# A hybrid decoder trunk on one core: where the writes of in_proj's weight pairs stand in the DMA queue

## The chip, the cores and the metric

The kernel runs on one core of one Trainium2 chip. The metric is the device time of one execution in microseconds (us), taken as the median of several runs; lower is better. Before the change it is 2620.64 us, the median of 3 runs (2617.64 to 2624.98).

## The reference

Two decoder layers on a sequence of 1024 tokens with a model width of 1024, in float32. Each layer normalises its input, multiplies it with one wide matrix w_in, and splits the columns of the product among three token mixers that work on the same input: A, a recurrence with a matrix state per head (RWKV-7); B, attention over dilated windows; C, latent attention. Their outputs are put side by side, multiplied with w_out and added to the residual. Then a gated feed-forward network follows:

```
for l in range(DEPTH):
    h = rms_norm(x, attn_norm_g[l])
    pa, pb, pc = split_sizes(h @ w_in[l], (A_PROJ, B_PROJ, C_PROJ))
    ya = rwkv7_mixer(pa, ...); yb = dilated_mixer(pb, ...); yc = mla_mixer(pc, ...)
    x = x + concatenate([ya, yb, yc]) @ w_out[l]
    h = rms_norm(x, ffn_norm_g[l])
    x = x + (silu(h @ w_gate[l]) * (h @ w_up[l])) @ w_down[l]
return rms_norm(x, final_norm_g)
```

## The kernel before, in words

**Split products.** A matmul of two float32 arrays is made of three passes over rounded parts. Each operand is split into a high part (a cast to fp32r on ACT, tile `wh` for weights) and a low part (source minus high part, on POOL for the weights here, tile `wl`). `mm3` (L268) multiplies high with high, high with low and low with high and adds all in PSUM. A weight tile of 128x512 values with its two parts is a *pair*; each part has 256 KB.

**in_proj** (L1154) computes h @ w_in for one half of the sequence (512 tokens) after the other, hf = 0 and hf = 1. Each half needs 36 weight pairs of the layer, two for each of 18 column blocks. For 16 of the blocks, a pair serves 4 steps of 3 matmuls with 512 columns (tile `inp`); the four pairs of the blocks 13 and 14 serve the values of mixer B (tile `vB`). Both halves use the same weights. So for hf = 0 a raw tile `wr` is loaded from `w_in`, split, used, and the pair is also written to a DRAM array `pairs_in`; for hf = 1 the pair is read back from there and needs no split (`again`, L477, is true for those keys).

**Planner.** The program is written out by a list scheduler, `Flow` (L111). Every activity is a generator, a *strand*, with a priority (lower goes first). A strand says which engine it wants next ("pe", "act", "pool", "dve" or "dma"), waits for an event, or asks for buffers. `run` (L173) always takes the strand that can start earliest by the planner's clocks, and `op` (L215) moves the clock of the engine by an estimated cost. The order in which strands are taken is the order of the instructions on each engine, and on the chip each engine works through its own instructions in that order. DMAs are issued by SP, in the order of the plan; `dma` (L324) estimates 256 KB at 728 ns (360 bytes per ns) on one clock for all DMAs, and the landing 2000 ns behind it. A DMA that must wait for a split on the chip holds up those behind it in SP's order.

**Loader.** `loader` (L482) supplies the weights in the order of their use. Its strand `fetch` (priority 1) loads raw tiles, at most three that are not yet split (`raws`, NRAW). The loader's own strand (priority 2) takes the raw tile, a slot of the ring (`ring`, NW = 6 pairs) and two pages of SBUF (`gp`, 79 pages in all, which the whole layer shares), and does the split. For in_proj's first half it then asks for the DMA and queues two writes, sets the event `there[k]`, which the read-back waits for, and sets `W[k]`, which in_proj waits for. After that it turns to the next pair. `drop` (L622) frees the two pages and the ring slot behind the last matmul with the pair.

**What lies around.** In layer 0, in_proj starts with the program, and its first half is accompanied by the norm of the second half (tiles `hx`, `hhi`, `hlo`), the token shift (`raw`, `pa`) and the beginning of the recurrence, which all use DVE, ACT and POOL. In layer 1 the loader's first splits lie beside the last matmuls of layer 0.

Of the kernel before, what the change touches and what calls it, by code (L numbers as in the profile page):

```python
# [36 lines left out]
C_SPLIT = (0, 1)  # L37
ROPE_START = (0, 16)
NORM_START = 8

VEC = {}
_n = 0
# [189 lines left out]
def trunk(ctx: ExitStack, tc: tile.TileContext, xT, pos, vec, con, first, w_in, small, uq, uqr, ukv,  # L232
# [91 lines left out]
    def dma(out, in_, nbytes):  # L324

        s = F.cur
        start = max(s.at(), F.clock["dma"])
        F.clock["dma"] = start + max(450.0, nbytes / 360.0)
        nc.sync.dma_start(out=out, in_=in_)
        return F.clock["dma"] + 2000  # L330
# [8 lines left out]
    def f32(ap):  # L339
        return ap.bitcast(F32)  # L340
# [140 lines left out]

    def loader(items):  # L482

        there.update({k: Event() for k, _ in items if k[0] in pairs_dram})

        def keep(k):
            late, soon = room(4), room(1)
            at = k[1][0][1] if k[0] == "S" else k[1]
            return lambda: soon() if k[0] == "in" or at < at_layer[0] else late()

        def own(k):

            rest, ffn = keep(k), k[0] in "gusS"
            return lambda: room(3.2)() if ffn and 3.2 in reserve else rest()

        def parts(k, srcs):

            if k[0] != "S":
                return [(Event(), srcs)]
            n = range(len(k[1]))  # L500
            at = [(g, 0) for g in n] + [(g, b) for g in n for b in (1, 2)] + [(g, 3) for g in n]
            return [(Event(), srcs[g][b], g, b) for g, b in at]

        def pair(k):

            return pairs_dram[k[0]][k[1], k[3], k[4]]

        queue = [(k, [] if again(k) else parts(k, srcs), own(k)) for k, srcs in items]

        def fetch():  # L510
            for k, todo, keep in queue:
                for ev, part, *_ in todo:
                    yield Need([raws])
                    wr = yield from page(["gp"], "wr", keep=keep, of=3.2)
                    w, t = 0, 0.0
                    yield "dma"
                    for a in part:
                        n = a.shape[-1]
                        t = dma(wr[:, w:w + n], a, 512 * n)
                        w += n  # L520
                    F.set(ev, wr, t)

        def raw_free(wr):
            free(wr)
            F.give(raws)

        F.spawn(fetch(), 1)
        for k, todo, keep in queue:
            if again(k):
                yield there[(*k[:2], 0, *k[3:])]  # L530
                yield Need([ring])
                w = yield from pages(["gp"], ["wh", "wl"], F32R, keep, 3.2)
                at = pair(k)
                yield "dma"
                for i in range(2):
                    t = dma(f32(w[i]), at[i], 262144)
                F.set(W[k], w, t)
                continue
            if k[0] == "S":
                gs = []  # L540
                for g, key in enumerate(k[1]):
                    evs = {b: ev for ev, _, g_, b in todo if g_ == g}
                    gs.append(Operands(key, k[2], evs, todo[0][1][0].shape[-1], keep, raw_free))
                for r in k[2]:
                    for g in gs:
                        yield from g.make(r)
                continue
            wr = yield todo[0][0]
            yield Need([ring])
            wh, wl = yield from pages(["gp"], ["wh", "wl"], F32R, keep, 3.2)  # L550
            yield from split(wr, wh, wl, "pool")
            raw_free(wr)
            now = F.cur.at()
            if k[0] in pairs_dram:
                yield "dma"
                for i, w in enumerate((wh, wl)):
                    t = dma(pair(k)[i], f32(w), 262144)
                F.set(there[k], None, t)
            F.set(W[k], (wh, wl), now)

    class Operands:

# [56 lines left out]
                F.spawn(self.later(2, a12), 2)  # L619
                yield from self.out(3, self.s2, free)  # L620

    def drop(w):  # L622
        free(*w)
        F.give(ring)

    def units(key, a):

# [385 lines left out]
    def layer(l):  # L1013
# [140 lines left out]
        def in_proj():  # L1154
            for hf in range(2):
                order = IN_ORDER[hf]
                for n_, idx in enumerate(order):
                    if hf == 0 and n_ == NORM_START:
                        F.spawn(norm1(1), 4)
                    if l == 0 and (hf, n_) == ROPE_START:  # L1160
                        F.spawn(rope_tables(), 7)
                    if hf == 1 and idx == B_START:
                        F.spawn(b_mixer(), 4)
                    if idx == 13:
                        for tb in range(2):
                            t = yield from page(["gp"], "pBv", keep=room(0.5))
                            for t2 in range(2):
                                tk = slice((2 * tb + t2) * 128, (2 * tb + t2 + 1) * 128)
                                p = yield from bank("vB", 4)
                                for k in range(KD):  # L1170
                                    hk = yield h[hf][k]
                                    wh, wl = yield W["in", l, hf, 13 + k // 4, k % 4 // 2]
                                    s = slice((k % 2) * 256, (k % 2) * 256 + 256)
                                    yield "pe"
                                    mm3(p[:, 0:256], (hk[0][:, tk], hk[1][:, tk]), (wh[:, s], wl[:, s]), k == 0, k == KD - 1)
                                    if tb == 1 and t2 == 1 and k % 2 == 1:
                                        drop((wh, wl))

                                def vout(p=p, t=t, t2=t2, tb=tb):
                                    if hf or l:  # L1180
                                        yield "act"
                                        acopy(t[:, t2 * 256:(t2 + 1) * 256], p[:, 0:256])
                                    else:
                                        yield rms
                                        yield "dve"
                                        ts(t[:, t2 * 256:(t2 + 1) * 256], p[:, 0:256], y0[:, 2 * tb + t2:2 * tb + t2 + 1], None,
                                           ALU.mult, rate=1.04)
                                    free(p)
                                    if t2 == 0:
                                        return  # L1190
                                    if hf == 1:
                                        F.set(Bv[2 + tb], t)
                                        return
                                    yield "dma"
                                    done = dma(pj_dram[8 + tb], t, 262144)
                                    F.cur.last, F.cur.t = None, done
                                    free(t)
                                    F.set(Bv[tb], (pj_dram[8 + tb], 128))

                                F.spawn(vout(), 2)  # L1200
                        continue
                    p = yield from bank("inp", 4)
                    for k in range(KD):
                        hk = yield h[hf][k]
                        wh, wl = yield W["in", l, hf, idx, k // 4]
                        s = slice((k % 4) * 128, (k % 4) * 128 + 128)
                        yield "pe"
                        mm3(p, (wh[:, s], wl[:, s]), hk, k == 0, k == KD - 1)
                        if k % 4 == 3:
                            drop((wh, wl))  # L1210
                        if n_ == len(order) - 1:
                            free(*hk)
                    if idx < 8:
                        F.spawn(shifted(hf, idx, p), 2)
                    elif idx == 8:
                        F.spawn(evac_to(Kr[hf], p, hf, 7, 64, shifted(hf, 8, p, 64, 96)), 2)
                    else:
                        ev, slot = {9: (Bq[0], 0), 10: (Bq[1], 1), 11: (Bk[0], 2), 12: (Bk[1], 3), 15: (Cq[0], 4),
                                    16: (Cq[1], 5), 17: (Ckv, 6)}[idx]
                        F.spawn(evac_to(ev[hf], p, hf, slot), 2)  # L1220
            unreserve(0.5)
            F.set(in_done)
# [1481 lines left out]
```

## Time and profile before

| | before |
|---|---|
| median of 3 runs | 2620.64 us |
| the profiled execution, its own time | 2621.2 us |
| its span, first to last instruction | 2619.4 us |
| mean granted clock of TensorE | 0.983 of full speed |
| PE busy | 2533.5 us, 97% of the span |
| DVE, ACT, POOL busy | 1747.4, 1135.3, 1154.9 us |
| DMA | 417.55 MB, mean 159 GB/s |
| writes to pairs_in, and reads from it | 144 each, 256 KB each |

The profiled execution is one among the executions of the kernel; its span leaves out what lies before the first and behind the last instruction. "Idle" is time in which an engine has no instruction running. A wait is put down to the operation that ended last before the waiting instruction could start; where an engine is not what sets the end, its waits cost nothing by themselves. Lines such as L295, L301 and L329 are those of helpers (the copy on ACT, the two-operand operation, and the DMA), so a row is told apart by its tiles.

### The profile page before, as it was taken

The numbers are of one execution on the slowest core, as the hardware profiler recorded it, in microseconds if no ns is written. First come the engines' busy times: TensorE is split into PE (matmuls) and PEld (weight loads), VectorE is DVE, ScalarE is ACT, GpSimd is POOL, SyncE is SP. The second block draws the span as 40 slices with busy tenths as digits, with TensorE's granted clock in tenths as the row PEclk, the third lists the DMA queues.
The fourth block names the chain that finished last, engine by engine and source line by source line (L and its number), as shares of the span: only waits on it lengthen the run. The fifth ranks groups of instructions, "written<-read, shape, count | busy, mean of one in ns | idle before, by whom it ended". The sixth has DMA issues, their size and how long they took to land. (4 is left out here: it accounts for less than half of the span.)

```text
span 2619.4 us, 38866 instructions
## 1 busy us (share of the span) xinstructions
PE 2533.5 (97%) x13112; PEld 2030.1 (78%) x13112; DVE 1747.4 (67%) x3415; ACT 1135.3 (43%) x2313; POOL 1154.9 (44%) x914
## 2 busy tenths in 40 slices
PE   7899999999899999999999999999998999999998
PEld 6678765888688888888878787568887888888887
DVE  6856677764987657566567376677458877665566
ACT  6542475663434334323354326557544334333221
POOL 3513231366645444455553123214655544444660
PEclk9999998999999999999999999999999999999999
DMA  7662321135255434896485241201461545449851
GB/s 265 234 211 88 118 64 29 56 115 199 99 176 194 140 134 161 307 316 229 166 290 194 93 171 36 63 25 53 168 198 60 197 165 177 147 136 351 291 196 65
DMA packets 235800, 417.55 MB, mean 159 GB/s; under 512 B 27600, under 2 KB 45264, under 8 KB 235472
## 3 DMA queue, kind: packets, MB, share of 16 engines
q1 hardware_dynamic: 235600, 415.07, 46.6%
q8 instruction: 103, 1.69, 0.3%
q14 instruction: 97, 0.79, 0.1%
HBM read 269.60 MB, written 141.69 MB: 157 GB/s over the span
## 5 line engine op out<-in xcount | busy, mean ns | idle before, releaser
L301 POOL TENSOR_TENSOR wl<-wr,wh 128x512 fp32r<-128x512 f32 (+1 forms) x304 | 436.5, 1448 | 387.0 <-ACT wh L295 310.2
L266 PE MATMUL gu<-hhi,wh 128*128 128x512 f32 x1232 | 483.7, 393 | 22.8 <-ACT u L295 16.5
L266 PE MATMUL gu<-hlo,wh 128*128 128x512 f32 x1232 | 481.1, 390 | 0.0
L266 PE MATMUL gu<-hhi,wl 128*128 128x512 f32 x1232 | 481.0, 390 | 0.0
L266 PEld LDWEIGHTS gu<-hhi,wh 128*128 128x128 f32 x1232 | 232.3, 189 | 79.6 <-ACT u L295 18.1
L295 ACT CAST wh<-wr 128x512 fp32r<-128x512 f32 (+1 forms) x424 | 244.4, 593 | 77.3 <-POOL wl L301 21.4
L266 PEld LDWEIGHTS gu<-hhi,wl 128*128 128x128 f32 x1232 | 232.3, 189 | 48.6
L266 PEld LDWEIGHTS gu<-hlo,wh 128*128 128x128 f32 x1232 | 232.4, 189 | 47.7
L301 POOL TENSOR_TENSOR wl<-s,wh 128x512 fp32r<-128x512 f32 (+1 forms) x136 | 181.5, 1342 | 197.1 <-ACT wh L295 142.8
L266 PE MATMUL dn<-bhi,wh 128*128 128x512 f32 (+1 forms) x664 | 252.0, 380 | 0.0
L266 PE MATMUL dn<-blo,wh 128*128 128x512 f32 (+1 forms) x664 | 251.5, 379 | 0.0
L266 PE MATMUL dn<-bhi,wl 128*128 128x512 f32 (+1 forms) x664 | 251.2, 379 | 0.0
L266 PE MATMUL inp<-hhi,wh 128*128 128x512 f32 x512 | 213.9, 418 | 11.4 <-ACT wh L295 11.4
L295 ACT CAST wh<-s 128x512 fp32r<-128x512 f32 (+1 forms) x204 | 116.8, 581 | 247.0 <-DVE s L301 199.7
L266 PE MATMUL inp<-hhi,wl 128*128 128x512 f32 x512 | 205.6, 401 | 5.2 <-POOL wl L301 5.2
L266 PE MATMUL inp<-hlo,wh 128*128 128x512 f32 x512 | 204.9, 400 | 1.2 <-DVE hlo L310 1.2
L301 DVE TENSOR_TENSOR x<-x,dn 128x512 f32<-128x512 f32 (+1 forms) x160 | 104.6, 657 | 109.3 <-PE dn L266 86.7
L301 DVE TENSOR_TENSOR v<-u,gu 128x512 f32<-128x512 f32 x132 | 90.1, 682 | 126.4 <-PE gu L266 126.2
L301 POOL TENSOR_TENSOR v<-v 128x512 f32<-128x512 f32 x66 | 98.0, 1488 | 134.3 <-DVE v L301 133.4
L291 ACT ACTIVATE P<-P,mx 128x512 f32<-128x512 f32 (+1 forms) x192 | 117.5, 613 | 63.9 <-DVE mx L857 42.5
L266 PEld LDWEIGHTS dn<-bhi,wh 128*128 128x128 f32 x664 | 124.9, 188 | 23.5
L266 PEld LDWEIGHTS dn<-bhi,wl 128*128 128x128 f32 x664 | 124.9, 188 | 23.4
(319 smaller groups left out, 5403.6 us busy)
## 6 DMA issues: line engine op xcount, KB each, us to landing
act_dram<-ahi SPq DMA_DIRECT2D x142, 256.0 KB
act_dram<-alo SPq DMA_DIRECT2D x142, 256.0 KB
bhi<-act_dram SPq DMA_DIRECT2D x142, 256.0 KB
blo<-act_dram SPq DMA_DIRECT2D x142, 256.0 KB
wr<-in_w_gate_dram SPq DMA_DIRECT2D x104, 256.0 KB
wr<-in_w_up_dram SPq DMA_DIRECT2D x104, 256.0 KB
wr<-in_w_in_dram SPq DMA_DIRECT2D x72, 256.0 KB
pairs_in<-wh SPq DMA_DIRECT2D x72, 256.0 KB
```

Of the source, the lines that this page charges most:

```text
L266: nc.tensor.matmul(out=out, lhsT=lhsT, rhs=rhs, start=start, stop=stop, **kw)
L291: nc.scalar.activation(out=out, in_=in_, func=func, **kw)
L295: nc.scalar.copy(out=out, in_=in_)
L301: ENG[eng].tensor_tensor(out=out, in0=a, in1=b, op=op)
```

## The change

After a split the loader no longer queues the two writes itself. It starts a strand of its own for them, `put` with priority 2, which begins 4000 ns behind the estimated end of the split, and goes on to the next pair. `drop` gets the pair's key: a pair that is written to DRAM is freed only when its write's estimated landing has passed, by a strand `drop_put`. `there` now holds only the keys that are written, so that pairs read back for the second half are freed as before.

```diff
+PUT_DELAY = 4000.0
@@ loader
-        there.update({k: Event() for k, _ in items if k[0] in pairs_dram})
+        there.update({k: Event() for k, _ in items if k[0] in pairs_dram and not again(k)})
@@
+        def put(k, w):
+            F.cur.after(F.cur.t + PUT_DELAY)
+            yield "dma"
+            for i in range(2):
+                t = dma(pair(k)[i], f32(w[i]), 262144)
+            F.set(there[k], None, t)
@@
             yield from split(wr, wh, wl, "pool")
             raw_free(wr)
-            now = F.cur.at()
             if k[0] in pairs_dram:
-                yield "dma"
-                for i, w in enumerate((wh, wl)):
-                    t = dma(pair(k)[i], f32(w), 262144)
-                F.set(there[k], None, t)
-            F.set(W[k], (wh, wl), now)
+                F.spawn(put(k, (wh, wl)), 2)
+            F.set(W[k], (wh, wl))
@@
-    def drop(w):
+    def drop(w, k=None):
+
+        if k in there:
+            F.spawn(drop_put(w, k), 2)
+            return
         free(*w)
         F.give(ring)
+
+    def drop_put(w, k):
+        yield there[k]
+        drop(w)
@@ in_proj
-                                        drop((wh, wl))
+                                        drop((wh, wl), ("in", l, hf, 13 + k // 4, k % 4 // 2))
@@
-                            drop((wh, wl))
+                            drop((wh, wl), ("in", l, hf, idx, k // 4))
```

## Rows read from the trace of the kernel before

**Rows 1.** The page, part 1: busy us of each engine (share) xinstructions.
```profile
PE 2533.5 (97%) x13112; PEld 2030.1 (78%) x13112; DVE 1747.4 (67%) x3415; ACT 1135.3 (43%) x2313; POOL 1154.9 (44%) x914
```

**Rows 2.** Busy us by stage; the last three: granted clock, DMA share, GB/s.
```profile
8.70:140.00 131.30, 117.78 (x571) 92.82 (x572) 102.66 (x200) 70.94 (x125) 66.92 (x54) 0.96 0.75 259
...
300.00:500.00 200.00, 193.35 (x1106) 132.24 (x1105) 147.37 (x444) 126.75 (x309) 64.86 (x61) 0.95 0.12 36
1290.00:1430.00 140.00, 135.56 (x692) 111.60 (x691) 103.72 (x210) 71.79 (x127) 74.15 (x57) 1.00 0.71 246
1600.00:1800.00 200.00, 189.85 (x1105) 129.16 (x1104) 140.49 (x442) 123.80 (x306) 62.69 (x59) 0.96 0.12 35
```

**Rows 3.** PE's waits, 8.7 to 140 us: us in total, times, longest.
```profile
PE inp L266 <- ACT wh L295: 11.4, 3, 8.7
PE inp L266 <- POOL wl L301: 5.2, 5, 2.1
```

**Rows 4.** Timeline of PE: start, us, operation, [idle before <-releaser].
```profile
33.09 0.50 PE L266 MATMUL inp<-hhi,wh 128*128 128x512 f32 x1 [1.42 <-ACT wh L295]
...
34.45 0.50 PE L266 MATMUL inp<-hhi,wl 128*128 128x512 f32 x1 [0.63 <-POOL wl L301]
...
102.71 0.50 PE L266 MATMUL inp<-hhi,wl 128*128 128x512 f32 x1 [2.13 <-POOL wl L301]
...
106.52 0.50 PE L266 MATMUL inp<-hhi,wh 128*128 128x512 f32 x1 [1.20 <-ACT wh L295]
...
109.09 0.80 PE L266 MATMUL inp<-hhi,wl 128*128 128x512 f32 x1 [1.84 <-POOL wl L301]
109.69 0.63 PE L266 MATMUL inp<-hhi,wh 128*128 128x512 f32 x1
...
114.81 0.41 PE L266 MATMUL inp<-hhi,wh 128*128 128x512 f32 x1
```

**Rows 5.** Busy us by stage of 20 us, columns as in rows 2.
```profile
100.00:120.00 20.00, 14.72 (x67) 10.78 (x66) 16.61 (x23) 7.02 (x12) 14.90 (x12) 0.83 0.56 194
120.00:140.00 20.00, 19.67 (x134) 17.95 (x132) 17.67 (x48) 5.16 (x8) 11.29 (x10) 1.00 0.97 335
```

**Rows 6.** Timeline of SP's DMA queue: start, us of issue, target<-source.
```profile
22.31 0.42 SPq L329 DMA_DIRECT2D wr<-in_w_in_dram  x1
...
24.79 0.89 SPq L329 DMA_DIRECT2D tabs<-in_con_dram  x1
...
90.93 0.42 SPq L329 DMA_DIRECT2D wr<-in_w_in_dram  x1
...
112.85 0.44 SPq L329 DMA_DIRECT2D wr<-in_w_in_dram  x1
...
139.17 0.73 SPq L329 DMA_DIRECT2D wh<-pairs_in  x1
```

**Rows 7.** Timeline of ACT: the casts of the 7th, 25th and 29th weight.
```profile
32.44 0.60 ACT L295 CAST wh<-wr 128x512 fp32r<-128x512 f32 x1
...
105.85 0.61 ACT L295 CAST wh<-wr 128x512 fp32r<-128x512 f32 x1
...
116.04 0.62 ACT L295 CAST wh<-wr 128x512 fp32r<-128x512 f32 x1 [0.67 <-DMA wr<-in_w_in_dram]
```

**Rows 8.** Timeline of POOL: the subtractions from 101.39 and from 128.24 us.
```profile
101.39 1.27 POOL L301 TENSOR_TENSOR wl<-wr,wh 128x512 fp32r<-128x512 f32 x1
...
128.24 2.56 POOL L301 TENSOR_TENSOR wl<-wr,wh 128x512 fp32r<-128x512 f32 x2 [4.63 <-DMA pairs_in<-wh]
```

**Rows 9.** Waits of SP's DMA queue, 8.7 to 140 us, columns as in rows 3.
```profile
SPq L329 <- ACT wh L295: 34.3, 19, 4.0
SPq L329 <- POOL wl L301: 21.4, 19, 2.6
```

**Rows 10.** ACT's waits for the loads, 8.7 to 140 us.
```profile
ACT wh L295 <- DMA wr<-in_w_in_dram: 7.4, 6, 2.2
```

**Rows 11.** Stages of PE's operations on tile inp alone.
```profile
0.00:148.70 148.70, 99.44 (x382) 0.97 0.77 262
```

## The prediction

> **What bounds the kernel now.** I read the page's busy shares first: PE is busy 2533.5 of 2619.4 us [rows 1], so only 85.9 us of idle can be won anywhere. Next the table by stage: in 8.7 to 140 us (layer 0, first half of in_proj) PE is busy 117.78 of 131.30 us, idle 13.5; in layer 1's like stage (1290 to 1430) it is idle 4.4 of 140 [rows 2]. Both stages make and write 36 weight pairs, so what the change can remove directly lies in the first. Then PE's waits in 8.7 to 140: 11.4 us for the cast wh and 5.2 us for the subtraction wl [rows 3]. Of the 11.4, 8.7 is the start of the program, before any weight exists, and stays. That leaves 2.7 + 5.2 = 7.9 us in which PE stood because a weight pair was not split yet. PE's timeline puts them: 1.42 us before 33.09 and 0.63 before 34.45 (2.05), then 2.13 before 102.71, 1.20 before 106.52 and 1.84 before 109.09 (5.17); the rest, 0.7, is in crumbs [rows 4]. After the last of these the matmuls start 0.427 us apart instead of 0.227 (12 starts between 109.69 and 114.81), the lower of the clock's two levels, 1.2 GHz: 12 x 0.2 = 2.4 us more [rows 4]; the granted clock from 100 to 120 us is 0.83 [rows 5].
>
> **Why the splits were late.** The seventh load of a weight was issued at 22.31, and its cast began only at 32.44; the 25th was issued at 90.93 and cast at 105.85 [rows 6, 7]. Where a cast does wait for its load, issue to cast is 3.2 us (112.85 to 116.04) [rows 6, 7]. So these weights had lain in SBUF some 7 and 11 us. It was the written order of ACT and POOL, not the DMA, that held them. In the code the loader strand asks for the DMA turn after each split, and only when the planner's DMA clock comes round goes on to the next split. Where the planner thinks its DMA backed up, other strands' work gets ahead of the cast. At 24.79 a transfer of 1088 KB was queued [rows 6]; at the planner's 360 bytes/ns that is 3.1 us of backlog, as an estimate, and the cast at 32.44 came behind ACT's work for the token shift.
>
> **The change part by part.**
> *Loader goes on at once.* No DMA turn between two splits. In the backed up opening that moves casts forward; I take the 2.05 us stall at 31.7 to 34.5 as gone. At 100 to 109 the DMA was busy only 0.56 [rows 5], so there the turn itself can hardly have held the loader. There POOL starts the subtraction at 101.39 without a gap before it, busy with other operations, and ACT casts only at 105.85 though its load had come long before [rows 7, 8]. These 5.17 us fall only if the loader comes to this place with more pairs in hand: the ring holds six, and two more pairs (2 x 12 matmuls x 0.227 = 5.4 us of PE work) would cover it. Bounds: 0 (same order, same stall) and 5.17 + 2.4 of clock. Loads (priority 1) now pass puts (priority 2) whenever the planner's DMA is backed up, so the lead should grow between 10 and 60 us; I take the full 7.6, the end that this priority speaks for.
>
> *Writes 4 us later.* The 144 writes of both layers stay, with the same bytes; nothing is saved on the 16 DMA engines. On SP's queue each write stood at the moment of its split: SP waited 34.3 us for wh and 21.4 for wl before 140 us [rows 9], and every load behind a write waited too. Those 55.7 us are no PE time: the casts waited for loads only 7.4 us in all [rows 10]. In layer 1 PE's idle in the like stage is only 4.4 us [rows 2], so I put layer 1 at 0; half of that idle, +-2, are the bounds.
>
> A rule of the Trainium skill would make more of this: "DMA: Bandwidth & Descriptors", section "Anatomy of one DMA — SWDGE (gpsimd) path", says that DMA engines never wait on semaphores, the issuing sequencer does before dispatch. By it all 55.7 us of SP's waits are time in which loads stood undispatched, and the sum would be some of that, up to the whole 13.5 us of idle. The trace agrees on where the wait sits, but its casts show that the loads were in time anyhow.
>
> *Pairs held for the write.* drop now waits for the put's estimated end, so a ring slot is kept at least 4.0 (delay) + 2 x 0.73 + 2.0 (the planner's figures) = 7.5 us behind the split. Six slots over 7.5 + 2 us of split give a pair each 1.6 us; the stage takes 131.3 / 36 = 3.6 us a pair. So the ring doesn't bind, until puts queue more than some 12 us behind.
>
> *Read-back for the second half.* The first read of a written pair was issued at 139.17 [rows 6], with the DMA 0.97 busy at 335 GB/s before it [rows 5]. Its first use is near 148.7: by then 382 of the first half's 384 matmuls of this form have started [rows 11], so the slack is about 9 us. That read needs a ring slot, and the last six pairs now hold theirs until their puts land. The pair six from the end is subtracted from 128.24, two in 2.56 us [rows 8], so it is split at 129.5. If nothing queues: 129.5 + 4.0 + 1.6 (0.52 MB at 335 GB/s) + 3.2 (landing as above) = 138.3, no loss. If all six puts queue: 129.5 + 4.0 + 6 x 1.6 + 3.2 = 146.3, read landed at 149.5, 0.8 us late. If the first half ends 9 us sooner the slack goes down by as much. Bounds 0 and 9; I take 0.7, since the slots' hold begins earlier too when the splits do.
>
> *The rest of the plan.* Every strand behind is planned anew. What this can do I bound by two stretches of equal work in different surroundings: 300 to 500 us is idle 6.65, 1600 to 1800 idle 10.15 [rows 2], 3.5 apart. I take 0, +-3.5 for one such stretch and +-6 for the kernel.
>
> **The sum**, against the profiled execution's own 2621.2 us (span 2619.4 and 1.8 around it): -2.05 - 5.17 - 2.4 + 0.7 = -8.9, so 2612.3. The median shown, 2620.64, is 0.56 below the profiled execution, so the forecast is **2612 us**, 0.33% faster.
>
> **The rivals.**
> *The stalls at 100 to 109 stay.* For: DMA busy 0.56 and weights long landed, so what orders ACT and POOL there is norm and recurrence work. Against: more lead from the opening. It keeps -2.05 and gives 0.7 back: 2619.
> *The change does not do what it says.* SP runs ahead of the estimated clock; if the chip lags the plan by more than 4 us, SP reaches the put before the split has ended and waits as now. For: plan and chip run apart freely. Against: the put is then behind loads that were planned after the split, so these are out already. 2620.6, no change.
> *ACT stands at casts (slower).* With no DMA turn between, a cast is planned at the load's estimated landing, 0.73 + 2.0 = 2.7 us behind issue, while the rows show 3.2 where a cast truly waited. ACT is in order, so 0.5 us and more at each cast falls on the evacuations and the recurrence behind it. Place: 10 to 140 us. Today 6 of 36 casts wait, 7.4 us in all, 1.2 each [rows 10]. If half of all 36 wait that long, 18 x 1.2 - 7.4 = 14 us of ACT; ACT is busy 70.94 of 131.3 us [rows 2], so perhaps two thirds of it, 9 to 10 us, reach PE, with the old stalls kept: 2630. It decides once PE's lead at these casts is under one pair (2.7 us). Against: the loads leave SP earlier too, no longer behind the puts.
>
> The same page of the Trainium skill, section "Latency and other measured facts", speaks for this rival: it puts HBM access at 0.2 us on average and 2 us at high load. No run here shows the memory's share alone; by it a landing could be near 2 us later than planned rather than 0.5, and the 18 casts would cost the more.
>
> **How the numbers follow.** Forecast (about 2612, faster) 0.42. Stalls stay 0.27 and no effect 0.10, both within 0.3%, which is 7.9 us and about what a measurement of this kernel can tell from no change. ACT stands at casts, or a late read-back with the new plan on top, 0.21, slower. So faster 0.42, same 0.37, slower 0.21. The forecast's own range is 2605 (the median less all 13.5 us of idle and 2.4 of clock) to 2618 (only the 2.05 won). The range that holds the time 8 times in 10 takes in the plan's -6 on the fast side, 2599 (2605 - 6), and the slow rival's 2630.
>
> **What would show it.** In the profile after: loads on SP's timeline no longer between a wh write and a wl write of the same pair, and SP's 55.7 us of waits for wh and wl mostly gone. PE's waits for wh and wl in 8.7 to 140 fall from 16.6 to under 10. The granted clock of 100 to 120 us is 1.00 instead of 0.83. The first read-back stands near 130 to 140 us with no PE wait at the second half's first matmuls. Layer 1's PE idle in the like stage stays near 4. The prediction is wrong if the stalls at 100 to 109 are there unchanged, if ACT's wait for the loads is well above 7.4 us, or if the time comes or goes in the stages behind 160 us by more than 6 us.

## The result: 2.6% slower, lost in one hole of layer 0

The changed kernel takes 2692.47 us (median of four runs, 2686.36 to 2694.58) against 2622.81 us of the kernel before (four runs on the same chip, three of them those of the forecast): ratio 1.0259, 95% interval 1.024 to 1.0277. The forecast of 2612 us, and its range, are wrong. The profiled execution has a span of 2692.4 us, 73.0 more than before, and PE's busy time, with the same number of instructions, is 25 us longer than in [rows 1]:

```profile
PE 2558.8 (95%) x13112; PEld 2058.4 (76%) x13112; DVE 1742.9 (65%) x3414; ACT 1132.6 (42%) x2311; POOL 1159.3 (43%) x914
```

More busy time for the same work means a lower clock somewhere. The table by stage shows where (columns as in rows 2):

```profile
8.70:140.00 131.30, 126.88 (x591) 105.30 (x592) 62.35 (x96) 59.77 (x114) 55.10 (x40) 0.99 0.92 321
...
100.00:120.00 20.00, 20.00 (x106) 17.25 (x105) 2.35 (x4) 1.24 (x2) 4.04 (x4) 1.00 0.99 338
...
180.00:200.00 20.00, 15.27 (x115) 13.03 (x113) 16.29 (x44) 4.89 (x10) 9.64 (x16) 0.98 0.08 19
200.00:220.00 20.00, 7.80 (x36) 5.91 (x36) 18.81 (x26) 2.30 (x4) 15.39 (x11) 0.50 0.12 37
220.00:240.00 20.00, 0.00 (x0) 0.00 (x0) 17.51 (x48) 1.04 (x1) 0.00 (x0) 0.50 0.13 43
240.00:260.00 20.00, 6.97 (x119) 6.60 (x120) 10.82 (x25) 3.27 (x6) 0.00 (x0) 0.50 0.06 14
...
1362.00:1502.00 140.00, 136.86 (x694) 113.27 (x693) 102.26 (x210) 71.43 (x127) 72.44 (x57) 0.99 0.70 244
```

The opening is better than before: from 8.7 to 140 us PE is idle 4.4 us instead of 13.5, and from 100 to 120 us it is never idle, at a granted clock of 1.00 [rows 2, 5]. Layer 1's like stage, which now stands 72 us later, is idle 3.1 of 140 (4.4 in [rows 2]). Between them PE has a hole: from 200 to 260 us it works 14.8 of 60 us at half the clock. Busy time multiplied by the granted clock says the same for longer stretches, as an estimate that takes work to go in step with the clock. Before:

```profile
0.00:160.00 160.00, 137.54 (x756) 109.21 (x756) 118.57 (x235) 79.53 (x140) 68.63 (x61) 0.97 0.77 264
160.00:300.00 140.00, 138.76 (x1036) 111.01 (x1034) 81.81 (x217) 52.83 (x102) 29.50 (x34) 0.99 0.36 122
```

After:

```profile
0.00:160.00 160.00, 146.38 (x676) 118.99 (x677) 79.27 (x149) 77.58 (x141) 59.50 (x51) 0.99 0.83 286
160.00:300.00 140.00, 89.58 (x651) 73.26 (x652) 82.16 (x183) 33.61 (x65) 32.56 (x35) 0.66 0.20 61
```

To 160 us it is 146.38 x 0.99 = 144.9 against 137.54 x 0.97 = 133.4 before, 11.5 ahead; from 160 to 300 us it is 89.58 x 0.66 = 59.1 against 138.76 x 0.99 = 137.4, so 67 us behind in sum at 300 us. That is nearly all of the 73.

PE's waits name what the hole waits for, 140 to 260 us in the first two lines; the last two are of 8.7 to 140, to be set beside [rows 3]:

```profile
PE mg L267 <- DVE T1Y L323: 36.1, 1, 36.1
PE bn L267 <- ACT bhi L296: 11.1, 1, 11.1
...
PE inp L267 <- ACT wh L296: 8.7, 1, 8.7
PE inp L267 <- POOL wl L302: 0.3, 1, 0.3
```

The weights are no longer waited for (the 8.7 is the program's start). What comes too late is mg, a step of the recurrence, for which DVE prepares the operand T1Y. So the next question is when the recurrence began. PE's operations by tile, of 0 to 800 us, give first and last start behind the three durations. Before:

```profile
L266 PE MATMUL lo<-xw,whi x4: 388/486/505, 40.8 to 173.7; 128*128 128x512 f32 x4
L266 PE MATMUL mg<-T1Y,Gm x128: 191/191/212, 155.2 to 290.9; 32*32 32x32 f32 x128
L266 PE MATMUL wo<-mhi,wh x128: 389/389/486, 561.5 to 654.9; 128*128 128x512 f32 x128
```

After:

```profile
L267 PE MATMUL lo<-xw,whi x4: 388/446/496, 146.6 to 157.2; 128*128 128x512 f32 x4
L267 PE MATMUL mg<-T1Y,Gm x128: 225/236/257, 253.0 to 373.5; 32*32 32x32 f32 x128
L267 PE MATMUL wo<-mhi,wh x128: 389/389/486, 636.9 to 726.7; 128*128 128x512 f32 x128
```

The recurrence's first matmul (lo) starts 105.8 us late, mg 97.8, and the out projection (wo) 75.4, about what the whole kernel loses. From there to the end hardly anything more is lost.

Its first matmul is late because of two loads. The strand `start` loads the tables (tabs, 1088 KB) and behind them the small matrix b, has ACT cast b to bones, and sets `tabs_done`, for which the recurrence waits. SP's queue and ACT's cast, before (rows not shown above; that of tabs is in [rows 6]):

```profile
27.82 0.35 SPq L329 DMA_DIRECT2D b<-in_con_dram  x1
...
35.57 0.30 ACT L295 CAST bones<-b 128x128 fp32r<-128x128 f32 x1
```

and after:

```profile
21.82 0.81 SPq L330 DMA_DIRECT2D swt<-in_small_dram  x2
...
105.05 0.42 SPq L330 DMA_DIRECT2D tabs<-in_con_dram  x1
110.83 0.38 SPq L330 DMA_DIRECT2D wh<-pairs_in  x1
...
131.60 0.33 SPq L330 DMA_DIRECT2D b<-in_con_dram  x1
...
138.07 0.30 ACT L296 CAST bones<-b 128x128 fp32r<-128x128 f32 x1
```

tabs is issued at 105.05 instead of 24.79, b at 131.60 instead of 27.82, bones is cast 102.5 us later, and lo follows. In SP's order of DMAs tabs is now the 128th instead of the 31st, b the 162nd instead of the 35th. The reason is in the code: the planner has one DMA clock, and while that clock stands ahead of the strands that wait for it, the one with the lowest number gets the turn. `start` has 7. Before, the loader's strand wrote its own pairs and could ask for one turn at a time, so there were moments without a better claim. Now each pair leaves a strand of priority 2 that waits for the DMA beside `fetch` (1). The DMA share is 0.99 at 338 GB/s from 100 to 120 us; tabs leaves behind the writes of 32 of the first half's 36 pairs, b behind those of all 36.

### The profile page after: what moved, and what is told of

Same layout as the page of the kernel before. It is cut to its first block, busy times and chain, and to the rows that moved or that the text cites. A ratio compares the mean times of both kernels' runs of the same rounds, so it can differ in the third digit from the quotient of the medians.

```text
span 2692.4 us, 38925 instructions
## 1 busy us (share of the span) xinstructions
PE 2558.8 (95%) x13112; PEld 2058.4 (76%) x13112; DVE 1742.9 (65%) x3414; ACT 1132.6 (42%) x2311; POOL 1159.3 (43%) x914
## 5 line engine op out<-in xcount | busy, mean ns | idle before, releaser
L267 PEld LDWEIGHTS dn<-blo,wh 128*128 128x128 f32 x664 | 124.9, 188 | 23.5
```

Of the source, the lines that this page charges most:

```text
L267: nc.tensor.matmul(out=out, lhsT=lhsT, rhs=rhs, start=start, stop=stop, **kw)
```

## Experiments

Theory A: the late loads make the loss. Rival B: the delay of 4 us, or the pairs held for it in the ring, makes it. Rival C: in_proj's second half runs ahead on PE, and ACT stands behind its evacuations. Later theory D was added for what A did not explain: any new plan of layer 0 has another length, and the one of before is a good one; its rival E was that write strands cost something there by themselves. Ratios are against the kernel before on the same chip, with 95% intervals; "load" is the last issue (us) of tabs, b and swt (small matrices that the recurrence needs too and that the strand `load_swt`, priority 3, loads); "mg to wo" the time from the first mg to the first wo of layer 0, both in the profiled execution.

| kernel | us | ratio | load | mg to wo | first wo |
|---|---|---|---|---|---|
| before | 2622.81 | 1 | 27.8 | 406 | 561.5 |
| after | 2692.47 | 1.0259 (1.024 to 1.0277) | 131.6 | 384 | 636.9 |
| before_late_tabs | 2697.98 | 1.0282 (1.0248 to 1.0316) | 132.7 | 392 | 645.4 |
| delay_0 | 2693.28 | 1.0261 (1.0231 to 1.0292) | 128.7 | 392 | 648.7 |
| start_first | 2662.71 | 1.0149 (1.0133 to 1.0165) | 103.5 | 374 | 604.5 |
| both_first | 2644.96 | 1.0078 (1.0056 to 1.01) | 22.9 | 429 | 593.2 |
| both_first_no_hold | 2646.3 | 1.0093 (1.0075 to 1.0111) | 22.5 | 427 | 594.7 |
| both_first_delay_0 | 2653.92 | 1.0117 (1.01 to 1.0135) | 22.6 | 429 | 594.4 |
| puts_between | 2650.01 | 1.0089 (1.0072 to 1.0106) | 24.1 | 432 | 593.7 |
| puts_last_0 | 2649.68 | 1.0095 (1.007 to 1.0121) | 24.8 | 430 | 590.1 |
| puts_last_1000 | 2633.05 | 1.0013 (0.9996 to 1.003) | 25.2 | 408 | 571.1 |
| puts_last_2000 | 2654.24 | 1.0109 (1.0088 to 1.013) | 24.9 | 430 | 596.8 |
| puts_last_3000 | 2640.86 | 1.0063 (1.0041 to 1.0085) | 24.8 | 414 | 585.2 |
| puts_last (4000) | 2647.06 | 1.0085 (1.006 to 1.0111) | 24.3 | 431 | 594.4 |
| before_first | 2642.73 | 1.0072 (1.0057 to 1.0087) | 22.8 | 432 | 584.9 |
| before_start_first | 2634.59 | 1.0026 (1.001 to 1.0041) | 25.1 | 415 | 571.8 |
| before_start_3 | 2637.15 | 1.0047 (1.0031 to 1.0063) | 30.1 | 414 | 574.4 |
| before_tabs_10 | 2639.72 | 1.0052 (1.0034 to 1.007) | 40.2 | 408 | 576.7 |

The first wo sorts the whole list almost as the ratio does: whatever a kernel loses, it has lost by there. Some win a part of it back behind: both_first's first wo is 31.7 us late, and the whole kernel loses 22.

### Are the late loads enough, and needed?

before_late_tabs: the kernel before, with the load held back alone. The pairs are written as before.

```
     def start():
...
+        F.cur.after(F.cur.t + 75000.0)
         yield "dma"
         dma(tabs_, con[:, NSMALL:NTABS], (NTABS - NSMALL) * 512)
```

> The kernel before with one thing: start asks for its DMA 75 us later, so that tabs and b come late; the puts are as they were. Theory A: the late loads alone are enough, the same hole in PE behind in_proj and a time of 2670 to 2710. Rivals B and C, in which the puts or the run ahead of in_proj are needed: within 10 us of the kernel before.

both_first: the changed kernel with both one-time loads ahead of all writes.

```
-        F.spawn(load_swt(), 3)
+        F.spawn(load_swt(), 1)
...
-    F.spawn(start(), 7)
+    F.spawn(start(), 1)
```

> The changed kernel with one thing more: the two strands that load what the recurrence needs (start: tabs and b; load_swt) have priority 1 instead of 7 and 3. Theory A (these loads lose every DMA turn to the new put strands, so that the recurrence of layer 0 starts 100 us late): tabs and b land near 25 us as before the change, the hole in PE at 190 to 260 us and the 1.2 GHz stretch to 290 go, the time is 2605 to 2622 us. Rival B (pairs held for the write take pages and ring slots from the recurrence): the hole stays whatever the priority of these loads, 2670 or more. Rival C (in_proj's second half runs ahead on PE, and ACT stands behind its evacuations): the hole stays, 2670 or more.

puts_last: the changed kernel, the same end from the other side.

```
-                F.spawn(put(k, (wh, wl)), 2)
+                F.spawn(put(k, (wh, wl)), 8)
```

> The changed kernel with the put strands at priority 8, behind all other strands, instead of 2. Nothing else is changed; start keeps 7. Theory A, if it is the puts that take the turns: tabs is issued early again, the hole is gone, 2600 to 2625. If it is the loads (priority 1) that take them: tabs late as in the changed kernel, about 2690. Rivals B and C: pairs are held as long or longer, so 2680 or more.

Without any write strand, the late load alone costs 1.0282, no less than the whole loss. SP's queue and PE's tiles of before_late_tabs:

```profile
53.96 0.44 SPq L329 DMA_DIRECT2D tabs<-in_con_dram  x1
132.69 0.63 SPq L329 DMA_DIRECT2D b<-in_con_dram  x1
...
L266 PE MATMUL lo<-xw,whi x8: 388/439/505, 150.3 to 1552.0; 128*128 128x512 f32 x8
```

Here tabs leaves at 53.96 and b only at 132.69, and lo starts at 150.3, against 146.6 in the changed kernel: the gate is the last of the two. Why tabs leaves so long ahead of b is not shown. The hole is not copied: from 200 to 260 us PE works 51.0 of 60 us here, and the deeper gap lies at 300 to 450 us, 109.2 of 150 at a clock of 0.80. The late start sets the loss; where PE then stands idle varies. With the loads early again, in two ways, 1.0259 falls to 1.0078 and 1.0085: 1.8 of 2.6%, some 47 of the 70 us. In puts_last only the writes have lost their place, and tabs leaves at 22.91, so it is the writes, not the loads of `fetch`, that take the turns. PE in the hole's place, in both_first:

```profile
200.00:260.00 60.00, 59.84 (x451) 47.05 (x450) 37.62 (x108) 17.38 (x38) 16.77 (x21) 1.00 0.17 54
```

So A is shown, in both directions, for that part. C falls with it, and so does the half of B on the pairs held, since both_first holds them as the changed kernel does. The other 20 us are not explained by A; the two do not simply add, as the late load alone already makes the whole loss.

delay_0 and start_first: the delay off, and half of the remedy.

```
-PUT_DELAY = 4000.0
+PUT_DELAY = 0.0
```

> The changed kernel with PUT_DELAY = 0: the strands of their own stay, the 4 us go. Theory A: the strands starve the loads, not the delay; tabs is still issued past 100 us, 2680 to 2700. If the delay is the cause: back to about 2620.

```
-    F.spawn(start(), 7)
+    F.spawn(start(), 1)
```

> The changed kernel with start alone at priority 1; load_swt stays at 3. In the written order of SP tabs is then early, but swt stands behind some 110 DMAs. Theory A (whichever load is lowest in priority loses, and the recurrence waits for both): the hole is back in full, 2680 to 2700, although tabs lands near 25 us. If it were tabs as a transfer (its 1.1 MB in the middle of the read-back) that cost the time: near both_first, 2645.

The other half of B falls: without the delay the time is the same 1.0261, and b is issued at 128.67. In start_first tabs and b go first, and swt, which left at 21.82 in the changed kernel, is now the one that loses its turn:

```profile
103.53 0.96 SPq L330 DMA_DIRECT2D swt<-in_small_dram  x2
```

lo starts at 120.9 instead of 146.6, and 1.0149 is left. The time is below what was expected, 2680 to 2700: a start 26 us sooner gave back 30.

### Where do the other 20 us come from?

before_first: the kernel before with the priorities of both_first and no write strand.

> The kernel before with start and load_swt at priority 1; its puts are as they were, inside the loader. This is the control for both_first, which left 22 us unexplained. Theory D (any shift in the opening makes a different plan for 160 to 590 us, and the one before was a lucky one): 2630 to 2650. Theory E (the 22 us come from the puts as strands, through the pairs' hold or the later read-back): within 8 us of 2621.

both_first_no_hold: both_first, and `drop` frees a pair at once, without waiting for its write.

```
     def drop(w, k=None):
 
-        if k in there:
-            F.spawn(drop_put(w, k), 2)
-            return
         free(*w)
         F.give(ring)
```

> both_first, but drop frees a pair behind its last matmul as in the kernel before, without waiting for the put (the page's next writer waits for the put on the chip). Theory E with the hold as the cause: the second half's matmuls of in_proj end near 343 us again instead of 382 and the time falls to 2615 to 2625. Theory D: another draw of the plan, anywhere in 2615 to 2655, the second half's end not tied to the hold.

both_first_delay_0: both_first with `PUT_DELAY = 0.0`.

> both_first with PUT_DELAY = 0. If the 4 us delay makes the 22 us (read-back late because the put is late): 2615 to 2625. If not: 2635 to 2655.

The control settles more than the two others: before_first, which has nothing of the change, loses 1.0072 though all its loads are early. Without the hold (1.0093) or the delay (1.0117) both_first is no faster, so neither is seen to cost its 20 us; as these are new plans too, a few us could hide in them. In before_first and both_first mg to wo takes 432 and 429 us instead of 406, while layer 1's took 425 and 423 (425 in the kernel before).

puts_last_1000, before_start_first, before_tabs_10 and puts_between: four more plans, each with loads early or nearly so. In the order named: puts at priority 8 and `PUT_DELAY = 1000.0`; the kernel before with start at 1; the kernel before with 10000.0 in place of the 75000.0 above; the changed kernel with puts at 4 and start at 3.

> The changed kernel with the puts at priority 8, behind start (7), and PUT_DELAY 1000: swt, tabs and b then stand in the first 22 of SP's DMAs, in the order of the kernel before, and pairs are still written by strands of their own. Theory A (late loads) plus theory D (layer 0 is planned anew whenever the opening changes, and before's plan is the better draw by about 20 us, mg to wo 406 us against 427 to 432): 2640 to 2650, mg to wo about 430. Rival E (strands for the puts themselves cost the 20 us in layer 0, by where their DMAs fall among the loads): the same 2640 to 2650, so this run alone doesn't part them. If the opening kept like before's is what matters: 2612 to 2622, mg to wo about 406, and the gain of the opening then shows.

> The kernel before, puts in the split's strand as they were, with start (tabs, b) alone at priority 1: tabs goes out ahead of swt and some 6 DMA rows sooner than before. Nothing is late and no strand is added. Theory D: the order behind it is another one, and mg to wo is 425 to 435 instead of 406: 2635 to 2650. If only late loads and put strands cost time: 2612 to 2625.

> The kernel before, with tabs held back by 10 us of the planner's time instead of 75: tabs is SP's DMA row 26 instead of 23, b row 39 instead of 27, swt stays. By the slope of the held-back kernel (75 us for 75 us, of which the recurrence loses what it starts late), 10 us late cost about 10: 2630 to 2636 without another draw. Theory D adds its 20 to 28 in layer 0: 2640 to 2655, mg to wo above 420.

> The changed kernel with start at priority 3 and the puts at 4, PUT_DELAY 4000 as it was: tabs is SP's DMA row 18, swt row 21, so nothing is late. Theory A with D: 2635 to 2650, mg to wo about 430, like the two others with early loads (2645, 2647). If the loads are the whole cause and the 20 us of those two came of the loader's place at priority 1: 2605 to 2620.

puts_last_1000 differs from puts_last in one number, the delay. SP's queue and PE's tiles of layer 0, of puts_last (4000):

```profile
21.57 0.81 SPq L330 DMA_DIRECT2D swt<-in_small_dram  x2
22.91 0.42 SPq L330 DMA_DIRECT2D tabs<-in_con_dram  x1
24.32 0.57 SPq L330 DMA_DIRECT2D b<-in_con_dram  x1
...
L267 PE MATMUL mg<-T1Y,Gm x128: 191/191/212, 163.8 to 291.8; 32*32 32x32 f32 x128
L267 PE MATMUL wo<-mhi,wh x128: 389/389/486, 594.4 to 684.2; 128*128 128x512 f32 x128
```

and of puts_last_1000:

```profile
21.73 0.81 SPq L330 DMA_DIRECT2D swt<-in_small_dram  x2
23.06 0.42 SPq L330 DMA_DIRECT2D tabs<-in_con_dram  x1
25.22 0.92 SPq L330 DMA_DIRECT2D b<-in_con_dram  x1
...
L267 PE MATMUL mg<-T1Y,Gm x128: 191/191/212, 162.9 to 301.5; 32*32 32x32 f32 x128
L267 PE MATMUL wo<-mhi,wh x128: 389/389/486, 571.1 to 664.5; 128*128 128x512 f32 x128
```

The loads leave within 1 us of each other, the first mg too, and wo starts 23 us apart. This could still be rival E, a cost that grows with the delay. The last runs part them: the delays 0, 2000 and 3000, and one more plan without write strands (start at 3 in the kernel before).

> Puts at priority 8, PUT_DELAY 0; swt, tabs and b among the first 21 DMAs of SP, as with 1000 and 4000. If put strands cost by their lateness: at or below the 2633 of 1000, 2620 to 2633, mg to wo 400 to 410. If the plan scatters: anywhere from 2615 to 2655, with mg to wo between 400 and 435.

> Puts at priority 8, PUT_DELAY 2000, loads as early. By lateness: between 2633 (1000) and 2647 (4000), about 2638, mg to wo about 416. If the plan scatters: anywhere from 2615 to 2655, and outside of 2633 to 2647 as likely as not.

> Puts at priority 8, PUT_DELAY 3000, loads as early. By lateness: about 2642, mg to wo about 423. If the plan scatters: anywhere from 2615 to 2655.

> The kernel before, without put strands, start at priority 3 instead of 7: tabs is SP's DMA row 17, b row 26, swt row 27, so all are as early as before. If put strands as such cost the 20 us: as before, 2620 to 2630, mg to wo about 406. If the plan scatters: 2615 to 2650, mg to wo 400 to 435 (with start at priority 1 and swt at row 24 it was 2635 and 415).

With the delay at 0, 1000, 2000, 3000 and 4000 the ratios are 1.0095, 1.0013, 1.0109, 1.0063 and 1.0085. There is no course in them: E's expectations for 0, 2000 and 3000 (at most 2633, about 2638, about 2642) were missed at two of three, 2649.68 and 2654.24. So a cost that grows with the delay does not show. The three plans without write strands and with early loads scatter as well, from 1.0026 to 1.0072.

before_tabs_10 does not belong among them, though it was meant as a draw: its b leaves 12.4 us late, mg starts 13.8 us late (169.0), mg to wo is 408 as before, and the loss is 12 to 14 us. That is the price of a late load again, and no scatter.

D in its first form, mg to wo of about 420 to 435 us in every new plan, was met by puts_between (432) and missed by puts_last_1000 (408), before_start_first (415) and before_tabs_10 (408). What stands is the weaker form in which the last expectations have it, and these were wide (2615 to 2655): once the opening is planned otherwise, layer 0 comes out longer by anything from nothing that can be told to 1.2%, with the change or without. That the new plan is the cause is argued from this, not shown.

A small cost of the write strands themselves is neither shown nor excluded. The mean of the eight with early loads, write strands and the hold is 1.0081, that of the three plans of before 1.0048, 0.3% apart, less than the scatter within each. But mg starts at 160.4 to 171.0 us in all nine kernels with write strands and early loads, and at 152.8 to 160.2 in the kernel before and the three. So of both_first's 31.7 us at the first wo, 9 have come up ahead of mg, in the opening, and only 23 between mg and wo.

What makes a plan long between mg and wo I could only narrow down. Below, PE's operations on tile inp alone, in 360 to 400 us: what is left of in_proj's second half beside the recurrence. puts_last_1000 (mg to wo 408):

```profile
360.00:400.00 40.00, 0.00 (x0) 0.00 (x0) 0.00 (x0) 0.00 (x0) 1.00 0.26 85
```

puts_last (431):

```profile
360.00:400.00 40.00, 4.87 (x18) 3.23 (x18) 0.00 (x0) 0.58 (x1) 1.00 0.18 58
```

In the plans of 406 to 415 us, 0 to 14 of these matmuls are recorded behind 360 us; in seven of the eight of 427 to 432 it is 18 to 24. The eighth, before_first, speaks against a rule: 432 us, and none. The link from the one to the other stays open. No kernel of the list beats the kernel before.

## Why the prediction was wrong

**The step that failed is "The rest of the plan".** It said "Every strand behind is planned anew" and took 0 with +-6. Two things were in that term. The first is the starved loads: 47 us. The part *Loader goes on at once* came close when it said that loads of priority 1 pass puts of priority 2 whenever the DMA is backed up. It did not ask which strands stand below 2. They were in the code and in the rows: [rows 6] show tabs itself on SP's queue at 24.79, and the text used that row only as a cause of backlog. The second is what a new plan of layer 0 leaves even with the loads early: 22 us in both_first, 3 to 31 over the kernels with write strands, all to the slow side, of a cause that stays open. The +-6 came from two stretches of one plan [rows 2]; these say nothing of another plan.

**The steps on the opening were right in the changed kernel, but partly for another reason.** Weight waits fell from 16.6 to 9.0 us, 8.7 of them the start; PE's idle time in 8.7 to 140 us fell by 9.1, of which 7.2 was forecast as weight stalls; the clock of 100 to 120 us went from 0.83 to 1.00. But PE had only in_proj to do, since the recurrence was not there: DVE was busy 2.35 us of 100 to 120 and ACT 1.24, against 16.61 and 7.02 in [rows 5]. With the recurrence back in its place, in both_first, PE waits for weights again:

```profile
PE inp L267 <- ACT wh L296: 9.0, 2, 8.8
PE vB L267 <- ACT wh L296: 3.0, 1, 3.0
...
PE vB L267 <- POOL wl L302: 1.0, 1, 1.0
PE inp L267 <- POOL wl L302: 0.9, 2, 0.6
```

That is 13.9 us, against 16.6 and 0.3 for vB before: 3 us won, not 7.2. From 100 to 109 us the stalls are gone, with PE at work 9.00 of 9 us (3.92 before), but most of the wait comes back a few us later:

```profile
115.06 0.39 PE L267 MATMUL vB<-wh,hhi 128*128 128x256 f32 x1 [3.01 <-ACT wh L296]
116.41 0.39 PE L267 MATMUL vB<-wl,hhi 128*128 128x256 f32 x1 [0.96 <-POOL wl L302]
```

PE's work of 8.7 to 140 us grows by 1.2 us in all, and the clock of 100 to 120 us is 0.93. So the lead put the stall off more than it covered it. (The 0.56 that the text gives for the DMA at 100 to 109 us is that of 100 to 120 [rows 5]; 100 to 109 alone has 0.42, which speaks for the same.)

**SP's waits** for wh and wl fell from 55.7 us [rows 9] to 14.7, in 8.7 to 140 us, as forecast:

```profile
SPq L330 <- POOL wl L302: 9.9, 11, 1.4
SPq L330 <- ACT wh L296: 4.8, 7, 2.6
```

The Trainium skill ("DMA: Bandwidth & Descriptors", "Anatomy of one DMA — SWDGE (gpsimd) path") has the issuing sequencer wait, not the DMA engine, and the trace agrees on the place. But 41 us less of such waits in the changed kernel went with 9.1 us more PE work, and with two loads that were needed standing behind writes that nobody waited for yet. In both_first these waits come to 32.0 us: of the 41, 24 are left once the recurrence is back.

**The pairs held and the writes later:** the hold costs nothing that can be told (1.0093 without it, 1.0078 with it), and layer 1's like stage is idle 3.1 us, within the +-2. **The read-back** was put at 138 to 146 us; it went out at 110.83, since in_proj had run ahead (383 matmuls on inp by 120 us, against 382 by 148.7 in [rows 11]), and no matmul of the second half waited for it. The 0.7 us were not there. With the recurrence back, in both_first, it went out at 136.35.

**The rivals.** *ACT stands at casts* did not come: ACT waits 8.9 us for raw weights there, in 3 waits, against 7.4 in 6 [rows 10], and that rival's two thirds of ACT's time had no row behind them (70.94 of 131.3 is 0.54):

```profile
ACT wh L296 <- DMA wr<-in_w_in_dram: 8.9, 3, 4.3
```

*No effect* and *stalls stay* were wrong too. Of the signs named, the last, "in the stages behind 160 us by more than 6 us", is the one that came true, and it should have had a mechanism beside it. The slow cases had 0.21 and reached 2630; kernels without a starved load go to 2654.

## What to carry to other kernels

When work moves to strands of its own, list every strand that competes for the same queue at a lower priority, and ask for each who waits for it: here a load of 64 KB held back a whole chain. Read a change's gain with the rest of the program in its place, since a stage can look better because its neighbour is missing. In a program written out by a planner, measure how far a neutral change of plan moves the time (here up to 1.2%) before a forecast of a few us is given.

## What the runs showed of the hardware

In the hole, with PE busy 7.8 of the 20 us from 200 to 220, the granted clock is 0.50, the lower of its two levels, 1.2 GHz, and it stays there after work has returned. The changed kernel, columns as in rows 2:

```profile
260.00:265.00 5.00, 4.55 (x35) 3.30 (x34) 0.42 (x1) 1.64 (x4) 0.00 (x0) 0.50 0.00 0
265.00:270.00 5.00, 5.00 (x40) 3.91 (x39) 0.57 (x2) 0.79 (x3) 0.61 (x1) 0.50 0.01 3
...
285.00:290.00 5.00, 5.00 (x31) 3.87 (x31) 0.99 (x3) 1.39 (x4) 0.61 (x1) 0.50 0.36 99
290.00:295.00 5.00, 5.00 (x40) 4.57 (x39) 0.57 (x2) 0.38 (x1) 0.62 (x1) 0.51 0.03 7
```

From 260 to 295 us PE is busy 34.55 of 35 us, the clock is 0.50 or 0.51, and from 300 to 320 us it is 1.00. Up to 17 us of those 35, as an estimate, are thus a cost of the hole that does not show as idle time. It is less where work does not take twice as long at half the clock: the first 128 matmuls of mg take 7.21 us of PE from 250 to 261 us, all at 0.50, and 4.41 us at 1.00 before, 1.6 times as long.
